# A second plain block at the start of a feed-forward stage, two inverse roots on VectorE, and a last chunk in two halves

## The chip, the core and the metric

The kernel runs on one core of a Trainium2 chip. The metric is the device time of one execution in microseconds (us), as the median over runs. The engines are TensorE (matmuls; its weight loads are recorded apart), VectorE, ScalarE, GpSimd and SyncE, which issues most DMAs; in the rows of the profile they are PE, PEld, DVE, ACT, POOL and SP.

## What is computed

One layer of a decoder trunk for 1024 prompt positions and 8 x 4 sample positions, which share the weights. The model's width is 1024 and the hidden width of a feed-forward net 2816.

```python
def swiglu(x, w1, w3, w2):
    return (jax.nn.silu(x @ w1) * (x @ w3)) @ w2

def trunk_layer(...):
    h = layer_norm(ALPHA * x + 0.5 * swiglu(x, f1_w1, f1_w3, f1_w2), ln1_g, ln1_b)
    z = h @ w_in + b_in
    ...  # windowed attention, chunked gated MLP, gates
    mix = (jax.nn.sigmoid(ga) * (att @ w_oa) + jax.nn.sigmoid(gb) * (yb @ w_ob)) @ w_out
    h = layer_norm(ALPHA * h + mix, ln2_g, ln2_b)
    h = layer_norm(ALPHA * h + 0.5 * swiglu(h, f2_w1, f2_w3, f2_w2), ln3_g, ln3_b)
    return h, new_bufs, vrows
```

## The kernel before

Activations are kept transposed: features on the 128 partitions, the 1056 positions as columns in four chunks (`NC`) of 264 (`C`). Every large matrix product is in float32r with both operands split into a high and a low part, and `mm3` issues three matmuls (high by high, high by low, low by high) for each block of 128 x 128 weights, 264 columns wide. So the splits (`split`: ScalarE casts the high part, VectorE subtracts for the low part) stand ahead of every product, for weights and for activations.

A feed-forward net (`ffn`, called with i = 0 for the first and in mode "out" for the second) has 22 hidden blocks (`FB`) of 128. Block 0 is done plainly: `hidden8` runs 48 matmuls for one chunk (24 for w3 by `units[1]` first, then 24 for w1 by `units[0]`), takes the Silu on ScalarE (L415) and the product on VectorE (L416), and stores the piece to memory (L417). The blocks 1 to 21 follow in `hidden`, a scheme of seven products of half-size pieces in place of eight, with 168 matmuls a block; `prep` (L355) loads and combines a block's weights one block ahead, on VectorE for the first and on GpSimd from block 3 on. The blocks in `PLAIN`, (0, 19, 20, 21), go to memory whole and are multiplied by w2 plainly in `out`; the rest are multiplied by w2 in the scheme of seven (`seven`), and `out` adds the plain part at the end, chunk after chunk: its `block(n, c)` is 12 matmuls for one of 8 feature blocks and one chunk, into one of three PSUM tiles "mm", which VectorE adds to the residual (L869). `unit` loads and splits one set of plain weights (128 x 1024) through two buffers for the raw data (`R`).

A layer norm runs chunk by chunk. `square_step` gathers squares as the blocks come, and `norm` (L581), a generator that other loops step on, does the rest: matmuls with a column of ones sum the squares over the partitions (L586, three matmuls that show as six passes), `rsqrt` takes the inverse root (ScalarE's Sqrt, then a reciprocal and one Newton step in three instructions on VectorE, L627 to L631), matmuls with the identity spread it over the partitions (L594), VectorE multiplies (L605, two instructions of 1056 elements), ScalarE or VectorE applies gain and bias (L613, L610). Then the chunk is split for the next product, or, in mode "out", stored (L619). Sums are centred before, so the mean does not appear here. The second norm's chunks end while the second feed-forward net begins: `ffn` drains the norm of chunk c right before `hidden8(units, 0, c)`.

In mode "out" chunk 2's multiply was held back until the norm of chunk 3 had been begun (`while ... NC - 1 not in self.lns`).

The order of the instructions on each engine is set by a scheduler under these generators, with priorities (`urgent`, `high_priority`, `chained`); each engine then works through its own queue in order.

Of the kernel before, what the change touches and what calls it, by code (L numbers as in the profile page):

```python
# [11 lines left out]

F32 = mybir.dt.float32
F32R = mybir.dt.float32r
AF = mybir.ActivationFunctionType
ALU = mybir.AluOpType
AX = mybir.AxisListType
# [3 lines left out]
P = 128  # L21
D = 1024
KB = D // P
# [19 lines left out]
EPL = EPS / ALPHA**2  # L43
# [19 lines left out]
SPREAD = 2  # L63
HOP = (4, 1, 4)
WARM = 2
FENCED = (mybir.EngineType.DVE, mybir.EngineType.Activation, mybir.EngineType.SP)
QKV = [s * 6 + 2 * g + hp for hp, g in HPG for s in range(3)]
GATES = [*range(34, 42), *range(26, 34)]
# [11 lines left out]
class Trunk:  # L80
# [471 lines left out]
    def square_step(self, c, n, tail=False):  # L552

        nc = self.nc
        tt = nc.vector.tensor_tensor
        y = self.Y[c][n // KH][:, n % KH]
        if n % 2 == 0 or tail:
            self.sq = self.M([P, 2, C])
        sq = self.sq
        if tail:  # L560
            s = self.sqs[c]
            if n == KB - 2:
                with self.urgent():
                    nc.scalar.activation(sq[:, 0], y, AF.Square)
                tt(s[:, 0], s[:, 0], s[:, 1], op=ALU.add)
                tt(s[:, 0], s[:, 0], sq[:, 0], op=ALU.add)
            else:
                with self.urgent():
                    tt(sq[:, 0], y, y, op=ALU.mult)
                    tt(s[:, 0], s[:, 0], sq[:, 0], op=ALU.add)  # L570
            return
        with self.urgent():
            nc.scalar.activation(sq[:, n % 2], y, AF.Square)
        if n == 1:
            self.sqs[c] = sq
        elif n % 2:
            tt(self.sqs[c], self.sqs[c], sq, op=ALU.add)

    def norm(self, c, i, mode, Y, s):
# [4 lines left out]
        pv = self.ax_tile()[:, :3]  # L584
        for j, o in enumerate(offs):
            nc.tensor.matmul(pv[:, j : j + 1], s[:, 0, o : o + P], self.ones[:, 0:1], start=True, stop=True)  # L586
        r, t = self.X([P, 3], "rs"), self.X([P, 3], "rt")
        self.rsqrt(r, t, pv, EPL)
        for _ in range(HOP[i]):
            yield  # L590
        pb = self.ax_tile()[:, :C]
        for j, o in enumerate(offs):
            lo = 0 if j < 2 else 2 * P - o
            nc.tensor.matmul(  # L594
                pb[:, o + lo : o + P], r[:, j : j + 1].to_broadcast([P, P]), self.ident[:, lo:], start=True, stop=True
            )
        yield
        while mode == "out" and c == NC - 2 and NC - 1 not in self.lns:
            yield
        if mode != "out":  # L600
            A = self.normed[c]
        cast = None
        for j in range(2):
            y = Y[j]
            nc.vector.tensor_tensor(y, y, pb.unsqueeze(1).to_broadcast([P, KH, C]), op=ALU.mult)  # L605
            for m in range(KH):
                n = KH * j + m
                g, b = self.vec(2 * i, n), self.vec(2 * i + 1, n)
                if c == NC - 1 and m % 2:
                    nc.vector.tensor_scalar(y[:, m], y[:, m], g, b, op0=ALU.mult, op1=ALU.add)  # L610
                else:
                    with self.tc.issue_after(cast) if cast else ExitStack():
                        nc.scalar.activation(y[:, m], y[:, m], AF.Identity, bias=b, scale=g)  # L613
            yield
            if mode == "out":
                parts = 2 if c == NC - 1 else 1
                for m in range(parts):
                    e = slice(m * KH // parts, (m + 1) * KH // parts)
                    nc.sync.dma_start(self.a["yo"][c, j][:, e], y[:, e])  # L619
            else:  # L620
                cast = self.split(*A[j], y)[0]
                nc.sync.dma_start(self.hD[i][c, j], y)
            yield

    def rsqrt(self, r, t, v, eps):
        tt = self.nc.vector.scalar_tensor_tensor
# [3 lines left out]
        tt(t, t, -0.5, r, op0=ALU.mult, op1=ALU.mult)  # L630
        self.chain = tt(r, t, 1.5, r, op0=ALU.add, op1=ALU.mult).ins  # L631

    def start_ln(self, c, i, mode):
        g = self.norm(c, i, mode, self.Y[c], self.sqs[c])
        self.lns[c] = g
        self.bg.append(g)

    def ffn(self, w13, w2p, w2, i, mode, resid):
        nc, preps = self.nc, {}
        last = FB + NG * (KB // 2) - 1  # L640

        def begin(f):
            if f < FB:
# [42 lines left out]
        def ready(f):  # L686
            for _ in preps.pop(f):
                pass
            if f < last:
                begin(f + 1)  # L690

        def between(f, bg):
            if f + 1 in preps:
                next(preps[f + 1], None)
            self.tick(bg)

        def load(n):
# [2 lines left out]
                while loads and total - len(loads) < n:  # L700
                    loads.popleft()()

        for f in range(1, FB):
            ready(f)
            if f == FB - 1:
                load(2)
            count = iter(range(1, 8))

            def after():
# [4 lines left out]
            self.hidden(f, after)  # L714
            del self.L[f]
        self.T = ({}, {})
        self.normed = [None] * NC
# [68 lines left out]
    def out(self, w2, i, mode, ready, between, load):  # L786
        nc = self.nc
        f = FB
# [68 lines left out]
        self.spare = True  # L857
        self.T, self.L = ({}, {}), {}

        def block(n, c):  # L860
            w = W2[n // NW]
            po = self.mm_tile()[:, :C]
            cc = slice(c * C, c * C + C)
            for k in range(NPL):
                hi, lo = H[k]
                self.mm3(po, w, k * NW * P + n % NW * P, hi[:, cc], lo[:, cc], k == 0, k == NPL - 1)
            y = self.Y[c][n // KH][:, n % KH]
            with self.urgent():
                nc.vector.scalar_tensor_tensor(y, po, HALF, y, op0=ALU.mult, op1=ALU.add)  # L869

        for c in range(NC):
            early = 6 if c == 0 else 0
            if mode != "out":
                self.hold_normed(c)
# [2 lines left out]
            for n in range(KB):  # L877
# [6 lines left out]
                block(n, c)  # L884
                if n >= early:
                    self.square_step(c, n, mode == "out" and c == NC - 1 and n >= KB - 2)
                self.tick(STEPS["out"])
            self.start_ln(c, i, mode)
        if mode == "out":
            self.drain()  # L890

# [883 lines left out]
```

## Time and profile before

| | us |
|---|---|
| median of three runs (2212.1, 2213.19, 2206.36) | 2212.1 |
| the profiled execution's own time | 2207.8 |
| its span in the trace | 2206.0 |
| mean granted TensorE clock over the span | 0.988 |

The second feed-forward net starts near 1485 us; block 1 of it begins at some 1510, the final additions of `out` run from about 2140 to 2192, and the tail of the last norm fills the rest. Line numbers in rows of the profile (L227) are those of the kernel. A row of the timeline shows start, length, engine, line, operation, output and inputs by the program's names, shape and count, and in brackets how long the engine idled before and who ended that. A window's row shows each engine's busy time in it, and PEclk, the share of its full clock that TensorE was granted.

### The profile page before, as it was taken

The numbers are of one execution on the slowest core, as the hardware profiler recorded it, in microseconds if no ns is written. First come the engines' busy times: TensorE is split into PE (matmuls) and PEld (weight loads), VectorE is DVE, ScalarE is ACT, GpSimd is POOL, SyncE is SP. The second block draws the span as 40 slices with busy tenths as digits, with TensorE's granted clock in tenths as the row PEclk, the third lists the DMA queues.
The fourth block names the chain that finished last, engine by engine and source line by source line (L and its number), as shares of the span: only waits on it lengthen the run. The fifth ranks groups of instructions, "written<-read, shape, count | busy, mean of one in ns | idle before, by whom it ended". The sixth has DMA issues, their size and how long they took to land.

```text
span 2206.0 us, 43143 instructions
## 1 busy us (share of the span) xinstructions
PE 2153.6 (98%) x17281; PEld 2101.2 (95%) x17281; DVE 1558.2 (71%) x2698; ACT 895.4 (41%) x1682; POOL 327.1 (15%) x238
## 2 busy tenths in 40 slices
PE   9999999999999999999989998998999999999997
PEld 8999999999999999999879887998999999999997
DVE  8776777657789636788575648778676676657787
ACT  5444444421126634344365444246444444421124
POOL 0433332100000011322000000000432332100000
PEclk9999999999999999999989999998999999999998
DMA  4445445596954335666844547513445545595832
GB/s 160 143 142 183 164 160 187 192 379 251 358 188 148 116 107 193 215 218 244 295 152 147 180 141 246 181 66 110 165 160 175 171 161 187 183 367 223 312 110 79
DMA packets 163640, 416.83 MB, mean 189 GB/s; under 512 B 24096, under 2 KB 60688, under 8 KB 160752
## 3 DMA queue, kind: packets, MB, share of 16 engines
q1 hardware_dynamic: 163008, 413.55, 53.9%
q8 instruction: 135, 2.21, 0.4%
q10 hardware_dynamic: 432, 0.54, 0.1%
q14 instruction: 65, 0.53, 0.1%
HBM read 301.64 MB, written 158.57 MB: 209 GB/s over the span
## 4 chain that ended last, share of the span: by engine, by line
PE 84%; DVE 5%; DMA 5%; issue 2%; ACT 1%; POOL 1%; SPq 0%; ACTq 0%; DVEq 0%; POOLq 0%
PE ax L227 43%; PE mm L227 36%; DMA M<-kv 2%; PE ax L1148 1%; DVE S L239 1%; DMA R<-wz 1%; PE ax L1171 1%; PE ax L1187 1%; DVE W L239 1%; DVE X L1330 1%; DMA S<-zD 0%; DMA S<-cD 0%; DVE M L1329 0%; DVE S L605 0%; POOL Q L370 0%
## 5 line engine op out<-in xcount | busy, mean ns | idle before, releaser
L227 PE MATMUL ax<-S,W 128*128 128x264 f32 x5472 | 716.9, 284 | 0.7 <-ACT S L978 0.6
L227 PE MATMUL mm<-S,W 128*128 128x264 f32 x5040 | 679.8, 290 | 22.6 <-DVE S L1489 9.5
L227 PEld LDWEIGHTS ax<-S,W 128*128 128x128 f32 x5472 | 686.1, 188 | 3.4 <-ACT S L978 2.1
L227 PEld LDWEIGHTS mm<-S,W 128*128 128x128 f32 x5040 | 642.3, 191 | 39.3 <-DVE S L1489 10.0
L227 PE MATMUL ax<-S,S 128*128 128x264 f32 x3288 | 485.1, 285 | 2.3 <-DVE S L987 2.2
L227 PEld LDWEIGHTS ax<-S,S 128*128 128x128 f32 x3288 | 434.8, 188 | 4.5 <-DVE S L987 3.5
L227 PE MATMUL mm<-S,S 128*128 128x264 f32 x2496 | 391.9, 287 | 5.9 <-ACT S L238 3.3
L227 PEld LDWEIGHTS mm<-S,S 128*128 128x128 f32 x2496 | 341.0, 190 | 7.5 <-ACT S L238 3.5
L238 ACT CAST W<-R 128x256 fp32r<-128x256 f32 (+2 forms) x172 | 127.9, 760 | 364.1 <-PE mm L227 135.0
L369 POOL TENSOR_TENSOR Q<-R 128x512 f32<-128x512 f32 x50 | 72.0, 1440 | 794.8 <-DMA R<-w13a 199.7
L239 DVE TENSOR_TENSOR W<-R,W 128x256 fp32r<-128x256 f32 (+2 forms) x172 | 149.6, 877 | 28.4 <-ACT W L238 28.0
L238 ACT CAST W<-Q 128x1024 fp32r<-128x1024 f32 (+1 forms) x79 | 77.7, 984 | 195.7 <-POOL Q L370 89.5
L444 DVE TENSOR_TENSOR S<-ax,M 128x264 f32<-128x264 f32 x84 | 33.4, 432 | 154.8 <-PE ax L227 151.7
L781 DVE SCALAR_TENSOR_TENSOR S<-ax,S 128x264 f32<-128x264 f32 x240 | 99.2, 428 | 59.1 <-PE ax L227 58.3
L239 DVE TENSOR_TENSOR S<-Q,S 128x1024 fp32r<-128x1024 f32 (+2 forms) x87 | 123.8, 1424 | 6.7 <-ACT S L238 6.4
L238 ACT CAST S<-Q 128x1024 fp32r<-128x1024 f32 (+2 forms) x87 | 86.2, 992 | 102.4 <-PE ax L227 71.4
L106 POOL CAST S<-ones 128x1 fp32r<-128x1 f32 x32 | 15.8, 508 | 753.8 <-DVE S L1567 364.9
L239 DVE TENSOR_TENSOR W<-Q,W 128x1024 fp32r<-128x1024 f32 (+1 forms) x79 | 91.9, 1163 | 24.2 <-ACT W L238 24.2
L239 DVE TENSOR_TENSOR S<-S,M 128x528 fp32r<-128x528 f32 x72 | 83.7, 1163 | 3.9 <-ACT M L238 2.3
L370 POOL TENSOR_TENSOR Q<-Q,R 128x512 f32<-128x512 f32 x50 | 83.7, 1675 | 2.7
L377 POOL TENSOR_TENSOR Q<-R,Q 128x512 f32<-128x512 f32 x50 | 81.8, 1635 | 1.2
L238 ACT CAST S<-R 128x512 fp32r<-128x512 f32 (+1 forms) x65 | 44.4, 686 | 92.5 <-DMA sumsA<-S 40.7
(199 smaller groups left out, 2066.5 us busy)
## 6 DMA issues: line engine op xcount, KB each, us to landing
ws<-st SPq DMA_DIRECT2D x144, 256.0 KB
S<-sumsA SPq DMA_DIRECT2D x63, 528.0 KB
S<-sumsB SPq DMA_DIRECT2D x63, 528.0 KB
M<-kv SPq DMA_DIRECT2D x96, 256.0 KB
sumsA<-M SPq DMA_DIRECT2D x90, 264.0 KB
sumsB<-M SPq DMA_DIRECT2D x90, 264.0 KB
R<-w13b SPq DMA_DIRECT2D x44, 512.0 KB
S<-zD SPq DMA_DIRECT2D x42, 528.0 KB
```

The source lines that it names most:

```text
L227: mm = lambda a, b, s, e: nc.tensor.matmul(o, a[:, cc], b, start=s, stop=e, skip_group_check=True)
L238: a = self.nc.scalar.copy(hi, src)
L239: b = self.nc.vector.tensor_tensor(lo, src, hi.bitcast(F32), op=ALU.subtract)
L369: tt(s12[:, lo], cd[:, lo], cd[:, hi], op=ALU.add)
L370: tt(s12[:, hi], s12[:, lo], ab[:, lo], op=ALU.subtract)
L377: tt(s34[:, hi], ab[:, hi], s12[:, hi], op=ALU.subtract)
L444: go(one, 5, False, lambda x: tt(h[:, x, 1], one[x], p7[:, x], op=ALU.add))
L781: nc.vector.scalar_tensor_tensor(y(x, r, e), bank[x], HALF, y(x, r, e), op0=ALU.mult, op1=ALU.add)
L1148: nc.tensor.matmul(pS[h][:, r, :nk], q[e, i * P : (i + 1) * P], k[e, k0 : k0 + nk], start=True, stop=True)
L1171: nc.tensor.transpose(pT[r][:, h, o], s[:, r, h, o], self.ident)
L1187: nc.tensor.matmul(pv[0][e, (i % 4) * P : (i % 4 + 1) * P], V[:, i - (nb - 1) + b, e], sT[:, r, h, b * P : b * P + P], start=b == 0, stop= ...
L1330: nc.vector.tensor_reduce(o, t, axis=AX.X, op=ALU.add)
```

## The change

First, in the second feed-forward net two blocks, 0 and 19, are done plainly at the start: for each chunk `hidden8` runs for block 0 and then for block 19, whose weights come through `unit`. Block 19 leaves the loop over the scheme of seven, and the loop goes over a list of blocks with a map to the next. The generator `s1` is stepped twice ahead of chunk 3 instead of being appended behind it.

Second, `rsqrt_dve` computes an inverse root on VectorE alone, in 11 instructions (a start from the bits of the number, three Newton steps). It is used for the last chunk of the second norm and for chunk 2 of the third. Behind the root of the second norm's chunk 2 stands a Silu of one element on ScalarE, into a tile that nobody reads.

Third, in mode "out" the last chunk is done in two halves of 132 columns, each with its own squares, root, spreading and stores, so its 96 matmuls of 264 columns become 192 of 132. The hold on chunk 2's multiply is gone. The number of 264-wide float32r matmuls in the program goes from 16296 to 16224.

```diff
 def norm(self, c, i, mode, Y, s, o, w):
-        offs = (0, P, C - P)
+        offs = [min(j * P, w - P) for j in range(-(-w // P))]
...
-        self.rsqrt(r, t, pv, EPL)
+        if c == NC - 1 and i == 1 or c == NC - 2 and mode == "out":
+            self.rsqrt_dve(r, t, self.X([P, 3], "rx", 1)[:, :cols], pv, EPL)
+        else:
+            self.rsqrt(r, t, pv, EPL)
+        if i == 1 and c == NC - 2:
+            nc.scalar.activation(self.X([P, 2], "warm", 1)[:, :1], r[:, :1], AF.Silu)
...
-        while mode == "out" and c == NC - 2 and NC - 1 not in self.lns:
-            yield
...
+    def rsqrt_dve(self, r, t, x, v, eps):
+        nc = self.nc
+        tt = nc.vector.scalar_tensor_tensor
+        nc.vector.tensor_scalar(x, v, eps, None, op0=ALU.add)
+        nc.vector.tensor_scalar(r.bitcast(I32), x.bitcast(I32), -0.5, MAGIC, op0=ALU.mult, op1=ALU.add)
+        for _ in range(3):
+            nc.vector.tensor_tensor(t, x, r, op=ALU.mult)
+            tt(t, t, -0.5, r, op0=ALU.mult, op1=ALU.mult)
+            self.chain = tt(r, t, 1.5, r, op0=ALU.add, op1=ALU.mult).ins
...
 def ffn(self, w13, w2p, w2, i, mode, resid):
+        plain = PLAIN[: 1 if i == 0 else 2]
+        blocks = [f for f in range(FB) if f not in plain] + [FB + g for g in range(NG * (KB // 2))]
+        after = dict(zip(blocks, blocks[1:]))
...
+            lead = [units] + [[self.unit(w13[f, x]) for x in range(2)] for f in plain[1:]]
             begin(1)
             for c in range(NC):
                 self.drain(lns.pop(c))
-                self.hidden8(units, 0, c)
-                if c:
-                    with self.chained():
-                        next(preps[1], None)
-            self.bg.append(s1)
+                if c == NC - 1:
+                    self.bg.append(s1)
+                    self.step(self.bg, 2)
+                for f, u in zip(plain, lead):
+                    self.hidden8(u, f, c)
+                    if c:
+                        with self.chained():
+                            next(preps[1], None)
...
-        for f in range(1, FB):
+        for f in blocks[: FB - len(plain)]:
...
 def out(self, w2, i, mode, ready, between, load):
-        for c in range(NC):
+        cuts = [(c, 0, C) for c in range(NC - 1)]
+        cuts += [(NC - 1, 0, C)] if mode != "out" else [(NC - 1, 0, C // 2), (NC - 1, C // 2, C // 2)]
+        for c, o, w in cuts:
```

How this moves instructions shows at three places. Up to the first of them, near 1480 us, the order is the same on all engines.

On ScalarE, around the first Silus of the second net, before (L613 gain and bias, L238 and L328 high parts, L415 the Silu of `hidden8`, L627 the root of chunk 3):

```order
L328 CAST S_17400<-S_17359 128x1056
L415 ACT_TABLE_LOAD
L415 ACTIVATE M_17576<-mm_17526 128x264
L238 CAST S_17096<-S_16333 128x1056
L328 CAST S_17434<-S_17402 128x1056
L328 CAST S_17468<-S_17357 128x1056
L328 CAST S_17500<-S_17436 128x1056
L627 ACT_TABLE_LOAD
L627 ACTIVATE X_17509<-ax_17505,eps_157 128x3
L415 ACT_TABLE_LOAD
L415 ACTIVATE M_17652<-mm_17602 128x264
```

And after, from the root of chunk 2 on (L644 is that root, L597 the Silu of one element, L240 the high parts of weights and activations; W_17518 and W_17525 are block 19's two units):

```order
L644 ACTIVATE X_17335<-ax_17331,eps_157 128x3
L597 ACT_TABLE_LOAD
L597 ACTIVATE X_17341<-X_17335 128x1
L240 CAST S_17283<-R_17282 128x1024
L575 ACTIVATE M_17459<-S_16331 128x264
L240 CAST W_17518<-R_17517 128x1024
L620 ACTIVATE S_16321<-S_16321,cols 128x264 x4
L240 CAST W_17525<-R_17524 128x1024
L575 ACTIVATE M_17459<-S_16331 128x264
L240 CAST S_17087<-S_16321 128x1056
L620 ACTIVATE S_16329<-S_16329,cols 128x264 x4
L330 CAST S_17395<-S_17354 128x1056
```

The table of the Silu is loaded behind chunk 2's root, and the one that chunk 3's root needed between two Silus is gone, as is the one that led back.

On VectorE at the same place, before (W_17523 is the low part of a raw piece of block 1; L323 are differences of activations for the scheme of seven):

```order
L323 TENSOR_TENSOR S_17359<-S_16331,S_17357 128x1056
L239 TENSOR_TENSOR W_17523<-R_17516,W_17522 128x1024
L577 TENSOR_TENSOR M_17303<-M_17303,M_17464 128x528
L323 TENSOR_TENSOR S_17402<-S_16331,S_16323 128x1056
L239 TENSOR_TENSOR S_17094<-S_16325,S_17092 128x1056
```

And after (W_17519 and W_17526 are the low parts of block 19's w1 and w3):

```order
L325 TENSOR_TENSOR S_17354<-S_16327,S_17352 128x1056
L241 TENSOR_TENSOR W_17519<-R_17517,W_17518 128x1024
L325 TENSOR_TENSOR S_17397<-S_16327,S_16319 128x1056
L241 TENSOR_TENSOR W_17526<-R_17524,W_17525 128x1024
L579 TENSOR_TENSOR M_17297<-M_17297,M_17459 128x528
L241 TENSOR_TENSOR S_17089<-S_16321,S_17087 128x1056
```

Block 19's second unit has come in behind the second difference; the low part of block 1's first piece comes later. On TensorE 26 matmuls stood between the spreading of chunk 3's root (L594) and the first matmul with chunk 3's split, and now 130 do, among them the plain blocks 0 and 19 of chunk 2.

On VectorE at the very end, before (from the last accumulation on; L605 with ax_25669 is chunk 2's multiply):

```order
L869 SCALAR_TENSOR_TENSOR S_22925<-mm_25739,S_22925 128x264
L569 TENSOR_TENSOR M_25753<-S_22925 128x264
L570 TENSOR_TENSOR M_25624<-M_25624,M_25753 128x264
L605 TENSOR_TENSOR S_22702<-S_22702,ax_25669 128x1056
L605 TENSOR_TENSOR S_22923<-S_22923,ax_25669 128x1056
L628 RECIPROCAL X_25772<-X_25772 128x3
L629 SCALAR_TENSOR_TENSOR X_25773<-ax_25768,X_25772 128x3
L630 SCALAR_TENSOR_TENSOR X_25773<-X_25773,X_25772 128x3
L631 SCALAR_TENSOR_TENSOR X_25772<-X_25773,X_25772 128x3
L605 TENSOR_TENSOR S_22817<-S_22817,ax_25779 128x1056
```

And after (the second half; L612 with ax_25944 is its multiply):

```order
L893 SCALAR_TENSOR_TENSOR S_22932<-mm_25918,S_22932 128x132
L568 TENSOR_TENSOR M_25793<-M_25793,M_25914 128x132
L571 TENSOR_TENSOR M_25932<-S_22932 128x132
L572 TENSOR_TENSOR M_25793<-M_25793,M_25932 128x132
L645 RECIPROCAL X_25938<-X_25938 128x2
L646 SCALAR_TENSOR_TENSOR X_25938<-ax_25935,X_25938 128x2
L647 SCALAR_TENSOR_TENSOR X_25938<-X_25938 128x2
L648 SCALAR_TENSOR_TENSOR X_25938<-X_25938 128x2
L612 TENSOR_TENSOR S_22824<-S_22824,ax_25944 128x4x132
L612 TENSOR_TENSOR S_22932<-S_22932,ax_25944 128x4x132
```

Chunk 2's multiply no longer stands ahead of the last reciprocal; it comes some 30 rows earlier, in the first half.

More of the change, by code (lines that the diff above doesn't have):

```diff
@@ L631, in rsqrt, with start_ln @@
         self.chain = tt(r, t, 1.5, r, op0=ALU.add, op1=ALU.mult).ins
-    def start_ln(self, c, i, mode):
-        g = self.norm(c, i, mode, self.Y[c], self.sqs[c])
+    def start_ln(self, c, i, mode, o=0, w=C):
+        g = self.norm(c, i, mode, [y[:, :, o : o + w] for y in self.Y[c]], self.sqs[c, o], o, w)
         self.lns[c] = g
@@ L688, in ready @@
                 pass
-            if f < last:
-                begin(f + 1)
+            if f in after:
+                begin(after[f])
         def between(f, bg):
-            if f + 1 in preps:
-                next(preps[f + 1], None)
+            if after.get(f) in preps:
+                next(preps[after[f]], None)
             self.tick(bg)
@@ L883, in out @@
                     W2.append(next(self.w2units))
-                block(n, c)
+                block(n, c, o, w)
                 if n >= early:
-                    self.square_step(c, n, mode == "out" and c == NC - 1 and n >= KB - 2)
+                    self.square_step(c, n, mode == "out" and c == NC - 1 and n >= KB - 2, o, w)
                 self.tick(STEPS["out"])
-            self.start_ln(c, i, mode)
+            self.start_ln(c, i, mode, o, w)
         if mode == "out":
```

56 lines of the change are left out of this document (30 added, 26 removed).

## The prediction

> **What bounds the kernel now.** I read the page first: the span and the share of each engine.
>
> ```profile
> span 2206.0 us, 43143 instructions
> PE 2153.6 (98%) x17281; PEld 2101.2 (95%) x17281; DVE 1558.2 (71%) x2698; ACT 895.4 (41%) x1682; POOL 327.1 (15%) x238
> ```
>
> TensorE is the bound over nearly all of the span, so a change is worth the TensorE time that it adds or takes, plus stalls of TensorE and the tail in which it has little to do. I looked next at the two places that the change touches, the start of the second FFN (1484 to 1528 us) and the end (from 2180 us), in the table of windows. Its columns: the window and its length; busy time and count of TensorE, its weight loads, VectorE, ScalarE and GpSimd; the granted clock; then DMA.
>
> ```profile
> 1494.50:1498.10 3.60, 1.72 (x13) 1.62 (x13) 3.34 (x4) 3.57 (x5) 0.00 (x0) 0.97 0.38 150
> 1498.10:1505.00 6.90, 6.90 (x35) 6.90 (x34) 4.48 (x9) 5.94 (x8) 0.00 (x0) 0.52 0.08 26
> 1512.60:1516.10 3.50, 0.27 (x3) 0.05 (x1) 3.50 (x7) 2.86 (x4) 0.00 (x0) 0.84 0.56 173
> 1516.10:1522.00 5.90, 5.82 (x25) 5.51 (x26) 5.87 (x8) 2.06 (x4) 0.00 (x0) 0.52 0.65 261
> 2179.90:2191.80 11.90, 11.90 (x100) 11.68 (x98) 8.01 (x18) 6.80 (x16) 0.00 (x0) 1.00 0.22 91
> 2191.80:2206.00 14.20, 2.22 (x12) 2.10 (x12) 7.93 (x15) 6.52 (x13) 0.00 (x0) 0.58 0.39 152
> ```
>
> TensorE stalls twice, and behind each stall the clock is halved (0.52) although TensorE is busy again. The timeline names the causes (start, length, engine, line; in brackets the idle time before, and who ended it).
>
> ```profile
> 1482.72 1.05 ACT L238 CAST S<-R 128x1024 fp32r<-128x1024 f32 x1 [2.31 <-PE mm L227]
> 1485.73 8.87 PE L227 MATMUL mm<-S,S 128*128 128x264 f32 x72
> 1494.74 1.28 ACT L415 ACT_TABLE_LOAD   x1
> 1496.48 3.86 PE L227 MATMUL mm<-S,S 128*128 128x264 f32 x21 [1.89 <-ACT M L415]
> 1509.11 0.73 PE L594 MATMUL ax<-ident,X 128*128 128x128 f32 x6
> 1516.12 0.81 PE L227 MATMUL mm<-S,S 128*128 128x264 f32 x2 [3.25 <-ACT S L238]
> 1526.89 1.72 PE L227 MATMUL mm<-S,W 128*128 128x264 f32 x12 [0.48 <-ACT M L415]
> ```
>
> The first stall waits for the first Silu, which stands behind the load of its table. The second is chunk 3: its norm is spread at 1509.11, and its split is there only at 1516.12. The x72 row also gives the pitch of a 264-wide matmul, 8.87 us / 72, less the overlap of the last: 0.122 us.
>
> **The change, part 1: the start of the second FFN.** The idle times in the brackets add up to 1.89 + 3.25 + 0.48 = 5.6 us. The half clock costs half of the time that was cold: a mean of 0.52 means that 96% of 6.90 and of 5.90 us were, so (6.6 + 5.7) / 2 = 6.1 us. Together 11.7 us can go. The Silu's stall goes because its table (1.28 us) now comes behind the root of chunk 2, near 1481, where ScalarE idles for 2.31 us, and because chunk 3's root on VectorE puts no other table between two Silus. Chunk 3's stall goes because TensorE then has 130 matmuls (15.9 us) between the spreading and chunk 3's first block, where it had 26 (3.2 us), and the split is ready 1516.12 - 1509.84 = 6.3 us behind the spreading. The seven more small steps of the root (11 for 4) are some 7 x 0.2 us of VectorE, inside the same cover; without it they would cost just that, 1.4 us. The price: block 19 done plainly is 4 x 48 = 192 matmuls for 168, so 24 x 0.122 = +2.9 us. What its preparation took on GpSimd lay beside TensorE and is worth nothing.
>
> What is late next is the weights of block 19, which are wanted right behind block 0's first chunk:
>
> ```profile
> 1483.98 3.42 DMA R<-w13b
> 1487.42 1.05 ACT L238 CAST W<-R 128x1024 fp32r<-128x1024 f32 x1 [3.33 <-DMA R<-w13b]
> 1488.37 2.10 ACT L613 ACTIVATE S<-S,cols 128x264 f32<-128x264 f32 x4
> 1489.98 1.22 DVE L239 TENSOR_TENSOR W<-R,W 128x1024 fp32r<-128x1024 f32 x1
> 1491.73 1.25 DVE L323 TENSOR_TENSOR S<-S,S 128x1056 f32<-128x1056 f32 x1
> ```
>
> In the new order the first unit's low part keeps VectorE's place at 1489.98; one difference of 1.25 us follows, then the second unit's low part of 1.22, ready near 1493.5. ScalarE casts that unit behind the four activations, by 1491.5. TensorE has finished block 0's first chunk at 1485.73 + 48 x 0.122 = 1491.6, may do two matmuls with the high part, and waits at the third: 1493.5 - 1491.8 = 1.7 us. Two buffers hold the raw units, so ScalarE and VectorE queue behind a third transfer too; chunk 1's split stands behind it, but is wanted only after another 48 matmuls (5.9 us). I take +2, with 0 and +6 as bounds: nothing, or another transfer of 3.42 us on top.
>
> Does the clock fall again? These windows, laid on its changes, show from where (1.00 or 0.50 is the granted clock):
>
> ```profile
> 1323.82:1327.23 3.41, 1.70 (x14) 1.00 1.04 239
> 1327.23:1330.64 3.41, 2.43 (x18) 1.00 1.00 334
> 1494.48:1497.89 3.41, 1.52 (x12) 1.00 0.40 159
> 1497.89:1501.30 3.41, 3.41 (x19) 0.50 0.13 44
> ```
>
> Behind 14 matmuls in 3.41 us it stayed, behind 12 it halved. A wait of 1.7 us leaves 14, so I count no halving, narrowly. Part 1: -11.7 + 2.9 + 2 = -6.8 us (from -10 to -3). [...]
>
> **Part 2: the last chunk in halves.** 96 matmuls of 264 columns (11.7 us) become 192 of 132. No matmul of this kind and width is in the trace. Three rows bound it: one-column matmuls, which leave nothing but the weights' load; 128-column ones with 64-column weights; and plain-f32 ones of 132 columns.
>
> ```profile
> 1479.38 0.72 PE L586 MATMUL ax<-ones,M 128*128 128x1 f32 x6
> L1187 PE MATMUL ax<-S,Q 128*64 128x128 f32 x280 | 24.5, 293 | 0.0
> L928 PE MATMUL ax<-M,M 128*64 128x132 f32 x12 | 2.6, 302 | 0.0
> ```
>
> The first is 0.112 us apart (start to start; 0.72 us for six holds the last one's drain), the second 24.5 / 280 = 0.088, the third 2.6 / 12 = 0.217. I take 0.112, the row with the same 128 x 128 weights: halving the columns saves almost nothing, as the weights must be loaded twice as often. 192 x 0.112 = 21.5 us, so +9.8. One more set of `ones` and `ident` matmuls (four passes each) lies within TensorE's work: 8 x 0.112 = +0.9. Bounds 16.9 and 41.7 us for the stage: +5.2 to +30. Chunk 2's multiply, no longer held back, is a pair of 2.4 us on VectorE, and three accumulators cover 3 x 12 x 0.112 = 4.0 us: nothing.
>
> **Part 3: the tail.** It runs from TensorE's last matmul through these rows:
>
> ```profile
> 2190.06 0.70 DVE L577 TENSOR_TENSOR M<-M,M 128x528 f32<-128x528 f32 x1
> 2191.83 0.43 DVE L869 SCALAR_TENSOR_TENSOR S<-mm,S 128x264 f32<-128x264 f32 x1
> 2192.30 0.43 DVE L569 TENSOR_TENSOR M<-S 128x264 f32<-128x264 f32 x1
> 2192.77 0.43 DVE L570 TENSOR_TENSOR M<-M,M 128x264 f32<-128x264 f32 x1
> 2193.12 2.41 DVE L605 TENSOR_TENSOR S<-S,ax 128x1056 f32<-128x1056 f32 x2
> 2193.35 0.80 PE L586 MATMUL ax<-ones,M 128*128 128x1 f32 x6 [1.55 <-DVE M L570]
> 2194.19 0.26 ACT L627 ACTIVATE X<-ax,eps 128x3 f32<-128x3 f32 x1 [3.53 <-PE ax L586]
> 2195.45 0.17 DVE L628 RECIPROCAL X<-X 128x3 f32<-128x3 f32 x1
> 2196.42 1.42 PE L594 MATMUL ax<-ident,X 128*128 128x128 f32 x6 [2.27 <-DVE X L631]
> 2197.88 2.42 DVE L605 TENSOR_TENSOR S<-S,ax 128x1056 f32<-128x1056 f32 x2 [1.60 <-PE ax L594]
> 2200.22 1.39 DVE L610 TENSOR_SCALAR S<-S,cols 128x264 f32<-128x264 f32 x4
> ```
>
> The reciprocal waited for chunk 2's pair of multiplies, 2195.45 - 2194.45 = 1.0 us: gone. The last pair, with half the columns, is two of 528 elements (0.70 each) for 2.41: -1.0. Three 264-wide steps at half width go from 0.43 to about 0.3, between 0.17 and 0.43: -0.4. Four passes for six, of the ones and at half clock of the spread: -0.2 - 0.5. The last gains and shifts: -0.3. Sum -3.4 (-2 to -4.5); the output's shorter pieces may take up to 1 of it back.
>
> **The sum.** -6.8 + 10.7 - 3.4 = +0.5 us on the profiled execution's 2207.8 us. That execution is 4.3 below the median of the runs (2212.1); the four shown average 2209.9, so I say 2210 us: no change. A difference within 0.3% (6.6 us) is about what a measurement of this kernel can't tell from none.
>
> **Rivals.** (A) The forecast, 2210 (2204 to 2217 by part 1's and the tail's bounds): 0.40.
>
> (B) Slower: the clock falls in the halves. A 132-wide matmul streams half of what a 264-wide one does in nearly the same time; a window of 3.41 us holds 30 at 0.112 us, which count as 15. Chunk 2's six one-column passes (0.67 us) now stand between halves and take six of these: 24, or 12 full ones, and 12 was the count that halved the clock at 1497.89. One-column passes seem not to count: that window, which held six of them, stayed cold though busy throughout. Against: 14 did not halve it, and 12 lies at the edge. From the trigger, some 45 matmuls in, weights take twice as long (half of 0.112 more a piece, then 0.21), and cold halves are too thin to warm it again: 140 x 0.1 = +14, so 2224 (2217 to 2229). It decides if one window holds all six passes and no full matmul: 0.29. [...]
>
> (C) Below some width this kind of matmul costs as the plain-f32 row, 0.217: 192 x 0.105 = +20, so 2230. For it is only that row, of another kind: 0.12.
>
> (D) Loading overlaps better than one-column rows show, 0.088 us: 192 x 0.024 = -4.6, so 2205: 0.09. Against it stands that its row has weights half as wide. [...]
>
> (E) Block 19's weights come later: a wait of 4 to 5 us, and two cold windows behind it as at 1498.10 (+3.3): 2217, 0.10. It decides if the wait leaves fewer than 14 matmuls in a window.
>
> **How the numbers follow.** The range must leave out 0.2: it drops C (0.12) and the lowest of A and D, so 2203 to 2229. Faster by over 0.3%: A's low end 0.08 and D's 0.04, 0.12. Slower: nearly all of B (0.28), C 0.12, half of E, and A's upper end (0.04), 0.49. Within: the remaining 0.39. A is the likeliest single case, though the slower ones together weigh more.
>
> **What would show it.** Part 1: no idle time of over 2 us for TensorE between the last `w_out` block and block 1, one near 1.7 ended by VectorE's split of a W, no ACT_TABLE_LOAD before a Silu there, and a clock of 1.00. Part 2: the last chunk's matmuls 0.112 us apart at clock 1.00, in some 22 us. Part 3: from the last matmul to the end some 11 us, with the reciprocal right behind the root. I am wrong if the granted clock in the last 25 us reads 0.5 (B), if the pitch there is 0.2 at full clock (C) or 0.09 (D), or if the first FFN or the mixing stage moves.

## The result, and the profile after

The changed kernel takes 2212.3 us (median of 22 runs, 2207.6 to 2216.8), the kernel before 2209.5 us in the same comparison (22 runs): a ratio of 1.0013 with a 95% interval of 1.0006 to 1.0020, so 2.8 us slower, 1.3 to 4.4. The forecast was no change (+0.5 us by its sum, 2210 us, range 2203 to 2229). The time is in the range and the difference within the 0.3% that was called no change, but the runs separate it from zero, and its sign is that of slower. The profiled execution took 2209.27 us; its page begins:

```profile
span 2207.5 us, 43428 instructions
PE 2159.7 (98%) x17405; PEld 2107.3 (95%) x17405; DVE 1558.0 (71%) x2728; ACT 891.7 (40%) x1685; POOL 319.1 (14%) x234
```

The windows of the changed kernel answer to those of before (the same columns): the start of the second net in three pieces, the two halves of the last chunk, and the tail.

```profile
1492.50:1494.50 2.00, 0.52 (x4) 0.30 (x3) 2.00 (x3) 2.00 (x4) 0.00 (x0) 1.00 0.98 288
1494.50:1511.00 16.50, 16.50 (x137) 16.50 (x138) 16.02 (x29) 9.16 (x14) 0.00 (x0) 1.00 0.44 149
1511.00:1528.00 17.00, 17.00 (x142) 17.00 (x141) 12.96 (x20) 6.77 (x11) 0.00 (x0) 1.00 0.52 179
2172.20:2184.30 12.10, 12.10 (x111) 12.10 (x110) 8.88 (x27) 6.40 (x17) 0.00 (x0) 1.00 0.23 93
2184.30:2196.60 12.30, 12.30 (x111) 12.22 (x110) 7.81 (x24) 7.69 (x19) 0.00 (x0) 1.00 0.22 89
2196.60:2207.50 10.90, 1.63 (x9) 1.45 (x8) 4.62 (x17) 2.23 (x6) 0.00 (x0) 0.61 0.35 99
```

TensorE is idle once for 1.5 us and then busy without a gap at full clock to 1528 us. Each half takes about as long as the whole chunk did (12.1 and 12.3 us of windows for 11.9), with TensorE busy throughout and the clock at 1.00. The timeline shows the one wait and the tail:

```profile
1492.48 0.51 PE L229 MATMUL mm<-S,W 128*128 128x264 f32 x2
1493.19 1.22 DVE L241 TENSOR_TENSOR W<-R,W 128x1024 fp32r<-128x1024 f32 x1
1494.47 2.79 PE L229 MATMUL mm<-S,W 128*128 128x264 f32 x21 [1.48 <-DVE W L241]
...
2198.39 0.58 PE L589 MATMUL ax<-ones,M 128*128 128x1 f32 x4 [1.72 <-DVE M L572]
2199.00 0.26 ACT L644 ACTIVATE X<-ax,eps 128x2 f32<-128x2 f32 x1 [2.08 <-PE ax L589]
2199.30 0.17 DVE L645 RECIPROCAL X<-X 128x2 f32<-128x2 f32 x1 [1.05 <-ACT X L644]
2200.27 0.99 PE L603 MATMUL ax<-ident,X 128*128 128x128 f32 x4 [1.30 <-DVE X L648]
2201.29 1.32 DVE L612 TENSOR_TENSOR S<-S,ax 128x528 f32<-128x528 f32 x2 [1.17 <-PE ax L603]
```

Two matmuls of block 19 run on the high part, and the third waits for VectorE's low part; in the tail the reciprocal follows the root at once, and the last pair of multiplies takes 1.32 us.

To see where the time went, I cut every trace at the same instructions: the ones of the second norm's chunk 2, the first gathering matmul of the second net, the last large matmul, the end. For the first two marks the rows of the changed kernel are these (before has them at 1479.38 and 2147.24):

```profile
1480.30 0.72 PE L589 MATMUL ax<-ones,M 128*128 128x1 f32 x6
2141.48 0.60 PE L533 MATMUL ax<-M,ones 128*128 128x264 f32 x2
```

The table has twelve traces, those of the experiments below among them; the thirteenth, e5, has other widths in its third segment. "Mixing" runs from the last ones of the first norm to the first mark; its program is the same in all. The first 727 us, up to there, are in the span alone.

| kernel | mixing | mark 1 to mark 2 | to the last large matmul | tail | span |
|---|---|---|---|---|---|
| before | 752.5 | 667.9 | 44.3 | 14.5 | 2206.0 |
| before, second execution | 752.7 | 666.2 | 44.3 | 14.5 | 2205.4 |
| before, third | 750.6 | 665.6 | 44.3 | 14.5 | 2203.4 |
| after | 753.3 | 661.2 | 54.9 | 11.1 | 2207.5 |
| after, second | 753.3 | 661.7 | 54.9 | 11.2 | 2207.3 |
| after, third | 751.8 | 661.6 | 54.9 | 11.2 | 2205.4 |
| e1: new start alone | 754.2 | 661.1 | 44.3 | 14.1 | 2200.5 |
| e2: halves alone | 760.4 | 667.4 | 54.9 | 11.6 | 2221.5 |
| e3: after, last chunk whole | 757.4 | 662.2 | 44.3 | 14.9 | 2205.6 |
| e4: after, tables back | 756.2 | 664.4 | 54.9 | 11.2 | 2214.2 |
| e6: other order | 755.8 | 661.2 | 44.3 | 14.9 | 2203.7 |
| e7: tables alone | 754.9 | 663.9 | 44.3 | 14.0 | 2204.3 |

The halves cost 54.9 - 44.3 = +10.6 us in every trace with halves, and the tail gives back 14.5 - 11.1 = 3.4. The new start is worth 667.9 - 661.2 = 6.7 us between the two executions first profiled, but 666.6 - 661.5 = 5.1 between the means of three.

### The profile page after: what moved, and what is told of

It is laid out like the page before. It is cut to its first block, busy times and chain, and to the rows that moved or that the text cites. A ratio compares the mean times of both kernels' runs of the same rounds, so it can differ in the third digit from the quotient of the medians.

```text
span 2207.5 us, 43428 instructions
## 1 busy us (share of the span) xinstructions
PE 2159.7 (98%) x17405; PEld 2107.3 (95%) x17405; DVE 1558.0 (71%) x2728; ACT 891.7 (40%) x1685; POOL 319.1 (14%) x234
## 4 chain that ended last, share of the span: by engine, by line
PE 86%; DVE 5%; DMA 5%; ACT 2%; POOL 1%; issue 1%; SPq 0%; ACTq 0%; DVEq 0%; POOLq 0%
PE ax L229 44%; PE mm L229 37%; DMA M<-kv 1%; PE ax L1174 1%; PE ax L1197 1%; DVE S L241 1%; PE ax L1213 1%; DMA R<-wz 1%; DVE W L241 1%; DMA S<-cD 0%; DMA zD<-M 0%; ACT S L240 0%; DVE X L1356 0%; DVE S L1515 0%; POOL Q L377 0%
## 5 line engine op out<-in xcount | busy, mean ns | idle before, releaser
L229 PE MATMUL mm<-S,W 128*128 128x264 f32 (+1 forms) x5256 | 702.4, 289 | 23.0 <-DVE S L1515 7.1
L229 PE MATMUL ax<-S,W 128*128 128x264 f32 x5400 | 707.4, 284 | 1.8 <-ACT S L1004 1.3
L229 PEld LDWEIGHTS mm<-S,W 128*128 128x128 f32 x5256 | 664.6, 190 | 39.5 <-DVE S L1515 9.1
L229 PEld LDWEIGHTS ax<-S,W 128*128 128x128 f32 x5400 | 677.0, 188 | 4.9 <-ACT S L1004 2.8
L229 PE MATMUL ax<-S,S 128*128 128x264 f32 x3240 | 477.2, 284 | 3.1 <-DVE S L1013 2.9
L229 PEld LDWEIGHTS ax<-S,S 128*128 128x128 f32 x3240 | 427.7, 188 | 5.3 <-DVE S L1013 4.3
L229 PE MATMUL mm<-S,S 128*128 128x264 f32 (+1 forms) x2520 | 389.7, 285 | 0.7 <-DVE S L893 0.7
L240 ACT CAST W<-R 128x1024 fp32r<-128x1024 f32 (+3 forms) x173 | 129.0, 761 | 362.6 <-PE mm L229 139.8
L241 DVE TENSOR_TENSOR W<-R,W 128x1024 fp32r<-128x1024 f32 (+3 forms) x173 | 151.2, 880 | 27.9 <-ACT W L240 27.7
L240 ACT CAST W<-Q 128x1024 fp32r<-128x1024 f32 (+1 forms) x78 | 76.7, 984 | 206.1 <-POOL Q L372 91.7
L240 ACT CAST S<-Q 128x1024 fp32r<-128x1024 f32 (+2 forms) x86 | 85.2, 991 | 98.6 <-PE ax L229 65.6
L108 POOL CAST S<-ones 128x1 fp32r<-128x1 f32 x32 | 15.8, 508 | 752.7 <-DVE S L1593 363.6
L240 ACT CAST S<-R 128x512 fp32r<-128x512 f32 (+1 forms) x64 | 43.8, 687 | 90.7 <-DMA sumsA<-S 43.5
```

The costliest lines, as they stand in the source:

```text
L108: self.nc.gpsimd.tensor_copy(t[:, 0, :1] if len(shape) == 3 else t[:, :1], self.ones[:, :1])
L229: mm = lambda a, b, s, e: nc.tensor.matmul(o, a[:, cc], b, start=s, stop=e, skip_group_check=True)
L240: a = self.nc.scalar.copy(hi, src)
L241: b = self.nc.vector.tensor_tensor(lo, src, hi.bitcast(F32), op=ALU.subtract)
```

## The experiments

Each result gives the median of the kernel's runs, and then the difference against the runs of before on the same chip (medians of 2208.1 for e1 to e4, 2208.0 for e6, 2207.7 for e7), worked out from the ratio and its 95% interval.

**One part alone, and one part undone.** e1 has the new start only: of the changed kernel it makes the last chunk whole, restores the hold, and leaves chunk 2's last root with Sqrt.

```diff
-        if c == NC - 1 and i == 1 or c == NC - 2 and mode == "out":
+        if c == NC - 1 and i == 1:
...
+        while mode == "out" and c == NC - 2 and NC - 1 not in self.lns:
+            yield
...
-        cuts += [(NC - 1, 0, C)] if mode != "out" else [(NC - 1, 0, C // 2), (NC - 1, C // 2, C // 2)]
+        cuts += [(NC - 1, 0, C)]
```

> The kernel before with only the new start of the second feed-forward net: plain blocks 0 and 19, the Silu of one element behind chunk 2's root, chunk 3's root of the second norm on VectorE; the last chunk is whole and chunk 2's multiply held back as before. By the prediction's part 1: 6.8 us faster than before (2202.7 against 2209.5), the clock at full from 1480 to 1530 us, one wait of 1.5 to 1.7 us. If the excess of the change (+2.8 us measured over 22 runs, +0.5 forecast) lies here, because the halved clock of before does not fall into every execution, the gain is only 4 to 5 us. If it lies in the halves, the gain is the full 6.8.

2204.8 us: -3.3 us (ratio 0.9985, 0.9975 to 0.9995), so -5.5 to -1.1. It is faster than before, and the changed kernel is slower. The forecast's 6.8 lies outside the interval.

e2 has the halves only (`s1` is appended behind the chunks again, which the cut at the end stands for):

```diff
-        if c == NC - 1 and i == 1 or c == NC - 2 and mode == "out":
+        if False:
...
-        if i == 1 and c == NC - 2:
+        if False:
...
-        plain = PLAIN[: 1 if i == 0 else 2]
+        plain = PLAIN[:1]
...
```

> The kernel before with only the last chunk in two halves and the hold on chunk 2's multiply gone (all roots with Sqrt, one plain block). By parts 2 and 3 of the prediction: +10.7 - 3.4 = +7.3 us, at a matmul pitch of 0.112 us. If in some executions the clock halves inside the halves (the rival with the clock), most runs are at +7 and some at +14 or more, with a mean clock lower by 0.003 or more in those; then the mean is +9 to +10. If the pitch or the tail were mis-sized, all runs move alike.

2216.8 us: +9.3 us (1.0042, 1.0026 to 1.0057). Its interval of 5.7 to 12.6 holds the forecast's 7.3. The part that is slower is the halves; in its trace, as in all with halves, the segment that holds them takes 54.9 us at full clock.

e3 is the changed kernel with only the last line of e1's diff, the last chunk whole:

> The changed kernel with its last chunk whole again: the new start, both roots on VectorE, no hold on chunk 2's multiply. By the prediction's terms: -6.8 us of part 1 and about -1.0 us since the last reciprocal does not wait for chunk 2's multiplies: -7.8 us, so some 2202 us, and the best of these kernels. If chunk 2's multiplies stall TensorE instead (over 2 us on VectorE between accumulations), -6.8 or less.

2205.6 us: -2.9 us (0.9987, 0.9975 to 0.9998), so -5.5 to -0.4, and the expected -7.8 lies outside. The new start falls short here as in e1, and what I expected of the hold did not come either: the tail is 14.9 us where before has 14.5. Its timeline says why:

```profile
2189.66 2.41 DVE L612 TENSOR_TENSOR S<-S,ax 128x1056 f32<-128x1056 f32 x2
2192.34 0.43 DVE L893 SCALAR_TENSOR_TENSOR S<-mm,S 128x264 f32<-128x264 f32 x1
2193.84 0.80 PE L589 MATMUL ax<-ones,M 128*128 128x1 f32 x6 [2.86 <-DVE M L572]
```

Without the hold the pair of multiplies falls just ahead of the last accumulation (L893), which starts 1.6 us behind the last matmul instead of 0.3. The pair moved from one place in the tail's chain to another.

**Which edit of the start does what.** e4 is the changed kernel with chunk 3's root by Sqrt and without the Silu of one element:

```diff
-        if c == NC - 1 and i == 1 or c == NC - 2 and mode == "out":
+        if c == NC - 2 and mode == "out":
...
-        if i == 1 and c == NC - 2:
+        if False:
```

> The changed kernel with chunk 3's root of the second norm by Sqrt again and without the Silu of one element, so that the three table loads of 1.28 us return to the first Silus. If the table loads are what the first stall was about, a stall of TensorE of about 1.3 us or more returns near the first hidden8 and the clock halves behind it, so 2 to 6 us slower than the change. If the plain blocks alone give cover (a product of block 0 is taken up only 96 matmuls later, and three accumulators are free), the table loads are hidden and the time is that of the change within 1 us.

2216.3 us: +8.8 us (1.0040, 1.0024 to 1.0056). That is 6 us more than the change's +2.8 by the runs, of which the trace shows half: mark 1 to mark 2 takes 664.4, or 2.9 more than after's mean of 661.5. The timeline has two new waits of TensorE, each behind a Silu that stands behind a table:

```profile
1500.13 1.28 ACT L417 ACT_TABLE_LOAD   x1
1501.87 1.96 PE L229 MATMUL mm<-S,W 128*128 128x264 f32 x14 [1.09 <-ACT M L417]
1508.24 1.28 ACT L417 ACT_TABLE_LOAD   x1
1509.98 3.17 PE L229 MATMUL mm<-S,S 128*128 128x264 f32 x24 [1.35 <-ACT M L417]
```

So three accumulators and 96 matmuls a chunk do not hide the tables. The clock, which I expected to halve behind such a stall, stayed at 1.00 from 1493 to 1530 us (24 matmuls in 3.17 us behind the second wait). One of its ten runs took 2231.6 us at a mean clock of 0.984, where the others had 0.989 to 0.992: that is 15 us, about the price of the rival with the halved clock. That run has no trace, so its cause stays open.

e7 has the two edits to the second norm's roots and nothing else: e1's diff, `plain = PLAIN[:1]`, and `s1` appended behind the chunks again.

> The kernel before with only the two edits to the roots of the second norm: the Silu of one element behind chunk 2's root and chunk 3's root on VectorE. One plain block, the last chunk whole, chunk 2's multiply held back. If each stall has the cause that the prediction gave it, the first one (1.9 us, and 0.4 to 0.5 at the next Silus) goes and the second, chunk 3's split, stays at 3.3 us or more with a half-clock stretch behind it: the stretch from chunk 2's ones to the first gathering matmul of the second net, 665.6 to 667.9 us in five executions of the old start and 661.1 to 662.2 in four of the new, reads 664 to 665, and the kernel is 2 to 3 us faster than before. If both stalls hang on the tables, it reads 661 or less, and the second plain block (+2.9 us of matmuls, 1.6 of waiting) bought nothing.

2206.1 us: -2.2 us (0.9990, 0.9981 to 0.9999), so -4.2 to -0.2, with 663.9 between the marks. The stalls, and the windows over the start (length, TensorE's busy time, granted clock):

```profile
1497.97 2.82 PE L229 MATMUL mm<-S,S 128*128 128x264 f32 x21 [0.65 <-ACT M L417]
1514.55 0.52 PE L229 MATMUL mm<-S,S 128*128 128x264 f32 x2 [3.29 <-ACT S L240]
1516.71 3.18 PE L229 MATMUL mm<-S,S 128*128 128x264 f32 x24 [0.18 <-DVE S L241]
1521.58 2.93 PE L229 MATMUL mm<-S,S 128*128 128x264 f32 x22 [1.69 <-DVE S L241]
1524.99 1.72 PE L229 MATMUL mm<-S,W 128*128 128x264 f32 x12 [0.48 <-ACT M L417]
```

```profile
1493.50:1511.00 17.50, 16.85 (x140) 1.00 0.27 84
1511.00:1530.00 19.00, 13.36 (x104) 1.00 0.53 177
```

Each stall answers to its own cause: the first shrank from 1.9 to 0.65 us, the second stayed at 3.3, with 1.7 us more behind it. But the waiting did not get less: the brackets add up to 6.3 us, where the three executions of before have 5.6, 6.8 and 6.0. What this trace lacks is the half clock, which I expected behind the second stall and which before has for 6.8 to 13.7 us. So the 2.7 us that the segment is shorter than before's mean (663.9 for 666.6) came from the clock, in one execution, and whether it stays full in others without those tables was not tested. The second plain block takes away the stalls that are left: another 2.4 us by the marks, net of its own 24 matmuls and its wait.

e6 is e3 with block 19's first chunk put behind block 0's second:

```diff
-                for f, u in zip(plain, lead):
-                    self.hidden8(u, f, c)
+                for j, x in {0: [(0, 0)], 1: [(0, 1), (1, 0), (1, 1)]}.get(c, [(0, c), (1, c)]):
+                    self.hidden8(lead[j], plain[j], x)
```

> The changed kernel with its last chunk whole and with block 19's first chunk put behind block 0's second, so that TensorE has another 48 matmuls (5.9 us) before it needs block 19's weights. The wait of 1.5 us ended by VectorE's split of W goes, and the clock is full from 1480 to 1530 us: 1.6 us better than the version with the whole last chunk (2205.6 in the same kind of comparison, -2.9 us against before), so some -4.5 us. If something else is late next in that place (chunk 2's split), nothing is gained.

2206.5 us: -2.7 us (0.9988, 0.9978 to 0.9998). Nothing gained; the rival in the expectation's last sentence was right in kind. The wait only changed hands:

```profile
1496.55 2.10 ACT L620 ACTIVATE S<-S,cols 128x264 f32<-128x264 f32 x4
1498.55 1.05 ACT L330 CAST S<-S 128x1056 fp32r<-128x1056 f32 x1
1499.52 0.38 ACT L417 ACTIVATE M<-mm 128x264 f32<-128x264 f32 x1
1499.94 2.95 PE L229 MATMUL mm<-S,S 128*128 128x264 f32 x22 [1.44 <-ACT M L417]
```

With all three accumulators full after 72 matmuls, TensorE waits 1.44 us for the first Silu, which stands on ScalarE behind gains and casts of the norm. ScalarE, not the weights alone, is late in this place.

**Does the half clock come in every execution?** The kernel before was profiled twice more, unchanged.

> The kernel before, unchanged, profiled in another execution. The new start alone gained 3.3 us (2.2 to both sides) where 6.8 was forecast. If the forecast was too high because it took both half-clock stretches (1497.9 to 1504.7 and 1515.0 to 1521.8 us, 6.1 us of loss) from one execution, then in this one at least one of the two is missing or shorter, while both stalls (1.9 and 3.3 us) are there again. If the halving belongs to the stalls, both stretches are there at the same length, and the missing 3.5 us lie elsewhere.

> The kernel before, unchanged, in a third execution, with the same question: where the half-clock stretches at the start of the second feed-forward net come and go from execution to execution, the mean over executions is what the new start can gain; where they are always there, it can't explain the miss.

The windows cover the whole start, 1493.5 to 1530 us, first of before, then of the second and of the third execution (length, TensorE's busy time, granted clock):

```profile
1493.50:1511.00 17.50, 15.62 (x105) 0.80 0.21 77
1511.00:1530.00 19.00, 15.20 (x101) 0.82 0.44 155
```

```profile
1493.50:1511.00 17.50, 15.16 (x124) 1.00 0.19 66
1511.00:1530.00 19.00, 14.50 (x97) 0.82 0.46 170
```

```profile
1493.50:1511.00 17.50, 15.50 (x115) 0.90 0.24 85
1511.00:1530.00 19.00, 14.99 (x108) 0.91 0.41 148
```

In the execution on which the prediction was built the clock was halved for 20% x 2 of 17.5 and 18% x 2 of 19 us, some 13.8 in all (13.7 by the trace's record of the clock); in the other two for about 6.9 (6.8 by that record, as in each of the two further traces that have the old start, e2 and e5). The timeline of the second execution shows what the full clock bought:

```profile
1497.56 2.83 PE L227 MATMUL mm<-S,S 128*128 128x264 f32 x21 [1.96 <-ACT M L415]
1504.72 3.19 PE L227 MATMUL mm<-S,S 128*128 128x264 f32 x24 [0.39 <-ACT M L415]
1515.47 0.81 PE L227 MATMUL mm<-S,S 128*128 128x264 f32 x2 [3.95 <-ACT S L238]
```

TensorE reached chunk 3 sooner and waited longer for it, 3.95 us for 3.25, and 0.39 us more for a Silu. The third execution, halved ahead of that wait like the first, has 3.25; e2 and e5, at full clock ahead of it, have 3.95 and 3.96. So the two losses are not independent: time lost to a half clock ahead of a wait for another engine is partly time that would have been waited. In the traces of before and after, the half-clock stretches up to the last additions last 3.41 or 6.83 us and start whole multiples of 3.41 us apart (before's at 1381.84, 1497.89 and 1514.96 us among them). In the second execution such a stretch starts at 1513.98 us, and the first stall has none behind it. These are windows of 3.41 us counted from that start, two at the first stall and two at the second:

```profile
1493.50:1496.91 3.41, 2.10 (x18) 1.00 0.44 173
1496.91:1500.33 3.42, 2.77 (x23) 1.00 0.17 57
1510.57:1513.98 3.41, 0.95 (x8) 1.00 0.59 184
1513.98:1517.39 3.41, 1.92 (x8) 0.50 0.85 341
```

The stall of 1.96 us lies in two of the windows and leaves 18 and 23 matmuls in them, and the clock stays at 1.00; the second leaves 8 in one, and the next reads 0.50.

The changed kernel was profiled twice more too:

> The changed kernel, unchanged, profiled in another execution. By segments of the traces the new start is worth -5.6 us (661.4 against 667.0, means of four and five executions), the halves +10.6 and the tail -3.4, so +1.6 in all, where the runs say +2.8 (1.3 to 4.4). If the rest is the mixing stage ahead of the change, whose length in the traces runs from 750.7 to 760.4 us with the same program, it reads more than 753 here, and the three segments read 661, 54.9 and 11.1 us again. If the halves sometimes run at half clock (the run with the lowest clock of another kernel with halves took 15 us more), the 54.9 reads 60 or more.

> The changed kernel, unchanged, in a third execution: the same question as in the second. Segments of 661, 54.9 and 11.1 us, and a mixing stage between 751 and 760 us, if the segments hold and the mixing stage is what varies.

The three segments came again (661.7 and 661.6, 54.9, 11.2), with no half clock in the start or the halves, and a mean clock over the span of 0.993 and 0.994. The mixing stage was 753.3 and 751.8, not longer than before's by more than its own scatter. In spans, three executions of each kernel differ by 2206.7 - 2204.9 = +1.8 us.

**Width, weights and the clock.** e5 is the kernel before with the last additions cut by chunk into one, two, three and four pieces:

```diff
+            parts = c + 1 if mode == "out" else 1
+            for j in range(parts):
+                e = slice(j * (C // parts), (j + 1) * (C // parts))
                 for k in range(NPL):
-                    hi, lo = H[k]
-                    self.mm3(po, w, k * NW * P + n % NW * P, hi[:, cc], lo[:, cc], k == 0, k == NPL - 1)
+                    hi, lo = (x[:, cc][:, e] for x in H[k])
+                    self.mm3(po[:, e], w, k * NW * P + n % NW * P, hi, lo, k == 0, k == NPL - 1)
```

> The kernel before, but the last additions by w2 of the second feed-forward net are done at other widths: chunk 0 at 264 columns a matmul, chunk 1 at 2 x 132, chunk 2 at 3 x 88, chunk 3 at 4 x 66, into the same accumulators. If the load of the 128 x 128 weights sets the pitch, it is 0.112 to 0.114 us at 132, 88 and 66 alike, and the stage takes 96, 192, 288, 384 matmuls at that pitch: 11.7, 21.7, 32.5 and 43 us, some +62 us in all. If streaming still counted, 88 and 66 would be shorter than 132. On the clock: if it goes by columns streamed in a window of 3.41 us (14 matmuls of 264 columns kept it, 12 and 11 did not), 30 matmuls of 88 columns count as 10 and of 66 as 7.5, so the clock halves early in chunk 2 and stays halved, the pitch there is 0.21, and it costs another 60 us. If it goes by whether TensorE is busy at all, it stays at 1.00.

2340.6 us, +133 against before's 2208.0; +122 was expected with the clock halved. The timeline has the first matmuls of the 132-wide and of the 88-wide chunk:

```profile
2154.39 9.71 PE L227 MATMUL mm<-S,W 128*128 128x132 f32 x85
2178.12 3.94 PE L227 MATMUL mm<-S,W 128*128 128x88 f32 x33
```

And the windows, over the 132-wide chunk and then from the first full window of 88 columns on (TensorE's busy time, granted clock; a count includes matmuls that only reach into the window):

```profile
2154.40:2178.10 23.70, 23.70 (x209) 1.00 0.08 31
2178.28:2181.69 3.41, 3.41 (x34) 1.00 0.25 94
2181.69:2185.10 3.41, 3.41 (x19) 0.50 0.00 0
2185.10:2238.80 53.70, 53.70 (x253) 0.50 0.05 21
2238.80:2323.20 84.40, 84.40 (x398) 0.50 0.00 1
```

At full clock the matmuls of 132 columns start 0.112 us apart (9.71 / 85 = 0.114 with the last one's drain), and so do the 31 of 88 columns that start in the first window. Behind that one window the clock reads 0.50, with TensorE busy all the time (3.41 of 3.41 us); it stays there to the end of the last additions, at 0.213 us a matmul for 88 as for 66 columns. So at these widths the pitch did not go by the columns; that the load of 128 x 128 weights, the same in all of them, sets it is what I conclude from the pitch of the one-column rows, 0.112 us as well. And TensorE being busy did not keep the clock: 31 matmuls of 88 columns filled a window, and 0.50 followed.

What rival (B) feared does happen, then, but at 88 columns: 132 held 1.00 in this trace (23.7 us) and in the changed kernel's (12.1 and 12.3 us). The first trace of the changed kernel even has the window that (B) asked for: it holds all six passes of the ones and not one 264-wide matmul (the same columns as the first windows of this document):

```profile
2175.11:2178.52 3.41, 3.41 (x33) 3.41 (x32) 3.27 (x9) 2.24 (x5) 0.00 (x0) 1.00 0.00 0
```

The clock stayed at 1.00 in it and behind it. 24 matmuls of 132 columns start in it, 3168 columns, where the 31 of 88 have 2728. As many columns are 12 matmuls of 264, the count that the prediction took to halve the clock. The traces of before and after have more such windows, whole multiples of 3.41 us from a half-clock stretch: of those at full clock between 1240 and 2150 us with 264-wide matmuls alone, the ones with 8, 11, 12 and 12 matmuls (counted as in the rows above, with those that only reach in) have 0.50 behind them, and those with 14 or more have 1.00. Counted so, the window above holds 27 matmuls of 132 columns, or 13.5 by (B)'s two for one, which was an estimate of mine: between the 12 and the 14. Whether two for one holds is not shown by these runs.

## Why the prediction was right or wrong

**The new start: the step that failed.** Its sum was -11.7 + 2.9 + 2. The price of the new start held: the wait for block 19's weights was 1.48 us (1.7 forecast), the clock stayed at 1.00, the stalls behind the table and for chunk 3 are gone, and 661.2 us between the marks is what -6.8 from that execution's 667.9 gives (661.1). What was mis-sized is the term that goes, -11.7: 5.6 us of stalls and 6.1 of half clock, both read from one execution and added. That one had twice the half clock of the four other traces with the old start, and the longest stretch of the five (667.9; the mean of the five is 667.0, and 666.6 for the three of before). In the second and the third execution the stalls come to 6.8 and 6.0 us, and 6.8 us of half clock cost at most 3.4: 10.2 and 9.4 at most, for 11.7. e2 and e5 show the same trade: as little half clock, but 7.5 and 8.0 us of stalls, and stretches of 667.4 and 667.8. So the gain is 5 to 5.5 us by the traces, and 3.3 (1.1 to 5.5) by the runs of e1. The slowdown is thus none of the rivals: it comes from the size of a term in the forecast's own sum. The low end that was given for this part, -10, does not come out of its bounds either: with no wait at all the sum is -8.8.

**The halves** cost what the sum said: 192 matmuls 0.112 us apart as forecast, +10.6 for +10.7. The row with the same weights was the right one of the three; C (0.217) and D (0.088) are out.

**The tail** gave 3.4 us as forecast, its half-width steps at 0.29 us (0.3), the last pair at 1.32 (1.4), the reciprocal right behind the root. That the sum is met to 0.1 us is in part luck: from the last pair's start to the end it saved 1.9 us where 1.3 were forecast, and the last accumulation, at 2197.21 us, starts 0.8 us behind the last matmul's start where before had 0.3, since VectorE had gains of the chunk's first half to do. The 1.0 us of the reciprocal came with the halves; that the lifted hold alone does not bring it, e3 shows.

**The rival with the clock** (B) did not decide: no trace with halves shows a half clock in them (54.9 us in all five), though the window that was to bring it was there, with 24 matmuls of 132 columns at 1.00. Its +0.1 us a matmul has no halves at half clock beside it; 88 columns took 0.213 us there for 0.112 at full clock. **The late weights** (E) did not come.

**What stays open.** By the traces the sum is -5.1 + 10.6 - 3.3 = +2.2 us, inside the measured 1.3 to 4.4. But the three segments of e1's trace say -5.9 where its runs say -3.3 with an end at -5.5, and the other five experiments with runs lean the same way, e4 most (+5.2 and +8.8). Their mixing stages were longer (754 to 760 us against 751 to 753) in single executions, and the changed kernel's was not. The record of the clock shows part of it: the mixing stages of these six traces have 23.9 to 30.7 us of half clock, those of before 17.1 or 20.5, those of the changed kernel 13.7 or 17.1. The changed kernel's runs scatter in the same sense, from 2207.6 us at a mean clock of 0.994 to 2216.8 at 0.988, and its three traces (0.993, 0.993, 0.994) lie at the fast end. Why a stage with the same program should have more of it in the experiments is not known, nor whether it is more than scatter.

## What to carry to other kernels

Cutting a matmul's columns buys little once its pitch hardly goes by them (0.122 us at 264, 0.112 at 132 and at 88): a last chunk in halves nearly doubled 11.7 us of matmuls to save 3.4 us of tail. A stall and the half clock behind it are read from several executions, not added from one, as the half clock at this start was 13.7 us in one execution and 6.8 in two others, and where it lay ahead of a wait, the wait was shorter (3.25 us for 3.95). When a wait is lifted, look for what stands next in the queue of the engine that ended it: here the weights' wait became a wait for a Silu of the same length.

## What the hardware showed that I had not expected

TensorE was busy throughout and lost half of its clock: behind one window of 3.41 us with matmuls of 88 columns on 128 x 128 weights it read 0.50 (e5), while with 132 columns it read 1.00 through 23.7 us. And a stall of 1.96 us that left 18 and 23 matmuls in two such windows had 1.00 behind it (the second execution of before), while one of 1.89 us that left 12 in one had 0.50 (the first).
